# A two-layer attention trunk on one Trainium2 core: one more value product by seven half products, and its combinations of x made earlier

## Chip, core and metric

One Trainium2 chip, of which the kernel uses one core. The time is the device time of one execution in microseconds. The engines are PE (TensorE, matmuls; PEld is its weight load), DVE (VectorE), ACT (ScalarE), POOL (GpSimd) and SP (SyncE, which here only issues DMAs).

## What is computed

A trunk of two layers on 512 tokens with 1024 features, all float32. Layer 0 is a forgetting attention, layer 1 a dilated attention of three groups with eight heads each; after each layer comes an embedding step with a gate. The reference, cut to what matters:

```python
def reference(x, p, ...):
    h = x
    for i in range(2):
        if i == 0:
            h = h + fox_mixer(rms_norm(h, fox_norm[0]), fox_w_in[0], fox_b_f[0], fox_w_out[0])
        else:
            h = h + dilated_mixer(rms_norm(h, dil_norm[0]), dil_w_in[0], dil_w_out[0])
        h = h + (p[i] @ ple_w_up[i]) * jax.nn.sigmoid(h @ ple_w_gate[i])
    return rms_norm(h, final_norm)

def dilated_mixer(h, w_in, w_out):
    proj = h @ w_in                  # q, k, v of 3 groups x 8 heads x 128, then a gate z
    ...
    for g, (window, dilation) in enumerate(((128, 1), (512, 4), (2048, 16))):
        o, l = dilated_window_attention(q[:, :, g], k[:, :, g], v[:, :, g], slopes[g], window, dilation)
    ...
    return (o * jax.nn.silu(z)) @ w_out
```

## The kernel before

Every matmul of float32 operands is done as three: each operand is split into a high part (ACT rounds it to the matmul's type) and a low part (DVE subtracts), and PE adds hi x hi, hi x lo and lo x hi in PSUM.

The weights come as a stream of granules of 512 KB (class `Stream`): SP loads them into four raw buffers `wraw`, ACT and DVE split them into five slots of `whi` and `wlo`. The program is written down as a list by a Python program. A planner then sets each engine's order: of what is ready by its own estimate, it takes what was written first. So work written later can run earlier. Between the steps of a product, side work can be written: `side.push(fn, lag)` puts a function off by so many steps (`tick`), and `side.flush()` writes all that is left.

The stretch around the change, in order:

- the second matmul of layer 0's gate (16 steps, `gate_evac(1)` with `to_dil` at its end for each block b of 128 tokens). `to_dil` normalizes `h` into `xn` and pushes two `transpose_to`, which write x transposed as `xn2T` (high and low) and a plain copy `xf`. Each pushed function makes four transposes on PE, two splits and a copy.
- `up_rows(1, ...)`, the second embedding's product `p[1] @ ple_w_up[1]`: eight steps of six matmuls of 512 columns. ACT copies each step's result to a tile `upo` (three buffers) and SP stores it to `up_dram`.
- `side.flush()`; the pool `mid0` is closed (with `xn`, `upo`, `pT` and others in it), and the pool `dil` is opened on its memory.
- the dilated layer's value products for the first half of the heads, (hf, g) = (0,0), (0,1), (0,2), then the products for q and k of head after head; later (1,0), (1,1), (1,2).

A value product by `token_rows` (L302 to L304) multiplies 512 tokens with 1024 features and 512 outputs: 96 matmuls of 512 columns from four granules. By `quad_rows` (L408 to L411) it is cut into 2 x 2 blocks and made of seven half products with 24 matmuls of 256 columns each, in this order: "11", "t2", "t1", "t3", "21", "t4", "22". Each takes a block or a combination of x (`xb`) and a block or a combination of weights (`Stream.quad`: a11, s2, s1, s3, a12, a22, s4, of which the s are made on DVE in the tiles `ws` and in the raw buffer). "11" lands in a bank that ACT copies to `p1`; "21" adds to the same bank. The other results pass through DVE adds into `u2`, `u4` and `v`. The combinations of x come from `combine_x`: four subtractions in place in `xf` and four splits into `comb`. Before, (0,0) and (1,0) run by `token_rows`, the other four by `quad_rows`, and `combine_x` is pushed during (0,0).

Of the kernel before, what the change touches and what calls it, by code (L numbers as in the profile page):

```python
# [15 lines left out]
F32 = mybir.dt.float32  # L16
# [6 lines left out]
P, T, D, KT, NB = 128, 512, 1024, 8, 4  # L23
# [10 lines left out]
def trunk_kernel(ctx, tc, x, p, fox_norm, fox_w_in, fox_b_f, fox_w_out, dil_norm, dil_w_in,  # L34
# [3 lines left out]
    base = ctx.enter_context(tc.tile_pool(name="base", bufs=1))  # L38
# [4 lines left out]
    def nm(s):  # L43
        uid[0] += 1
        return f"{s}_{uid[0]}"
# [154 lines left out]
    g_fo = [tok_granules(fox_w_out[0], c * 512) for c in range(2)]  # L200
    g_g0 = [tok_granules(ple_w_gate[0], c * 512) for c in range(2)]
    g_up1 = [ws.add(ple_w_up[1], 0, 2, c * 512, 512) for c in range(2)]
    QUADS = ((0, 1), (0, 2), (1, 1), (1, 2))
    g_dv, g_dq, g_dk, g_dz = {}, {}, {}, {}
    z_after = {0: (0, 1), 2: (2, 3), 4: (4, 5), 7: (6, 7)}
    for hf in range(2):
# [38 lines left out]
    side = Side()  # L245
# [13 lines left out]
    def drive(main, steps=1, at={}):  # L259


        for i, _ in enumerate(main):
            side.tick()
            step(steps if isinstance(steps, int) else steps[i])
            if i in at:
                at[i]()
# [8 lines left out]
    def token_rows(act, granules, lhs, evac, group=1, nk=KT, halves=False):  # L275

        tiles = [None] * NB  # L280
        assert not halves or group >= len(granules)
        ng = len(granules)
        for g0 in range(0, ng, group):
            parts = {}
            for b in range(NB):
                if tiles[b] is None:
                    tiles[b] = bank(tok[b])
                end = g0 + group >= ng
                cols = ((0, 256), (256, 512)) if halves and b == NB - 1 and end else ((0, 512),)
                for c0, c1 in cols:  # L290
                    for gi in range(g0, min(g0 + group, ng)):
                        if gi not in parts:
                            parts[gi] = ws.get(granules[gi])
                        wh, wl = parts[gi]
                        if gi == 0 and c0 > 0:
                            tiles[b] = rotate(tr)
                        o = tiles[b][:, c0:c1]
                        for kk in range(2):
                            k = 2 * gi + kk
                            xh, xl = lhs(act[0], k, b), lhs(act[1], k, b)  # L300
                            first, last = k == 0, k == nk - 1
                            PE.matmul(o, xh, wh[:, kk, c0:c1], start=first, stop=False)  # L302
                            PE.matmul(o, xh, wl[:, kk, c0:c1], start=False, stop=False)  # L303
                            PE.matmul(o, xl, wh[:, kk, c0:c1], start=False, stop=last)  # L304
                        if gi == ng - 1:
                            if len(cols) > 1:
                                evac(b, o, c0, c1)
                            else:
                                evac(b, o)
                        yield  # L310
# [145 lines left out]
    def transpose_to(act, k0, b, src, copy=None):  # L456

        t = rotate(tr)
        for i in range(4):
            PE.transpose(t[:, i * P:(i + 1) * P], src[:, i * P:(i + 1) * P], ident)  # L460
        tv = t.rearrange("p (k n) -> p k n", k=4)
        split_out(act[0][:, k0:k0 + 4, b * P:(b + 1) * P],
                  act[1][:, k0:k0 + 4, b * P:(b + 1) * P], tv)
        if copy is not None:
            ACT.activation(copy[:, k0:k0 + 4, b * P:(b + 1) * P], tv, AF.Copy)
# [54 lines left out]
    def up_rows(L, pool, pT, granules):  # L520

        for c in range(2):
            def evac(b, t):
                u = pool.tile([P, 512], F32, tag="upo", bufs=(8, 3)[L], name=nm("upo"))
                ACT.activation(u, t, AF.Copy, scale=0.5)
                store = lambda c=c: SP.dma_start(up_dram[L][b][:, c * 512:(c + 1) * 512], u)
                if L == 0:
                    stores.append(store)
                else:
                    store()  # L530
            yield from token_rows(pT, [granules[c]], blk, evac, nk=2)

    stores = []
    with tc.tile_pool(name="start", bufs=1) as sp:
# [47 lines left out]
        for n, _ in enumerate(token_rows(xnT, g_v[0], blk, v_evac(0), group=4)):  # L582
# [3 lines left out]
            if n > 7:  # L586
                with tc.issue_after(last["load"].ins):
# [7 lines left out]
                       base=0, pattern=[[-1, P]], channel_multiplier=1)  # L595
    qk = base.tile([P, 8, T], F32R, tag="qkh", bufs=1, name="qk")
# [299 lines left out]
    def to_dil(b, mp, h, ss, gain, hg):  # L896
        if b == 0:
            xn2T.append(act_pair("xn2T"))
        SP.dma_start(h_dram[b], h[:, b, :])
        rstd = rstd_of(mp, ss)  # L900
        xn = mp.tile([P, D], F32, tag="xn", bufs=2, name=nm("xn"))
        DVE.scalar_tensor_tensor(xn, h[:, b, :], rstd, gain, OP.mult, OP.mult)
        for c in range(2):
            side.push(lambda c=c: transpose_to(xn2T[0], 4 * c, b, xn[:, c * 512:(c + 1) * 512], dil_in["xf"]), 10)

    mid = ExitStack()
    mp, pT1 = mid_layer(0, ozT, g_fo, g_g0, lambda b: rows(x[0])[b], fox, dil_norm, to_dil)
    drive(up_rows(1, mp, pT1, g_up1))
    side.flush()
    mid.close()  # L910


    dil = ExitStack()
    dp = dil.enter_context(tc.tile_pool(name="dil", bufs=1))
    xT = xn2T[0]

    qk = base.tile([P, 8, T], F32, tag="qkh", bufs=1, name="qk2")
    d0, d1, d2 = dil_in["dist"]
    slope = lambda g, j: 2.0 ** (-8.0 * (g * 8 + j + 1) / 24)
    scale = 128 ** -0.5  # L920

# [2 lines left out]
    comb = [a.rearrange("p k n -> p (k n)") for a in act_pair("comb")]  # L926
    for i in range(4):
        xb[f"t{i + 1}"] = [a[:, 1024 * i:1024 * (i + 1)].rearrange("p (k n) -> p k n", k=4) for a in comb]

    def by_block(d):  # L930

        return lambda h: (d.rearrange("p (b r i) -> p r b i", b=4, r=4)[:, 2 * h:2 * h + 2],
                          lambda t: t.rearrange("p (r b i) -> p r b i", r=2, b=4))

    def by_residue(d):
        return lambda h: (d[:, 256 * h:256 * h + 256], lambda t: t)

    def combine_x():

        xf = dil_in["xf"]  # L940
        b11, b12, b21, b22 = (xf[:, 4 * i:4 * i + 4, 256 * h:256 * h + 256] for i in range(2) for h in range(2))

        def less(d, a, b):
            return lambda: DVE.tensor_tensor(d, a, b, OP.subtract)

        def parts(n, d):
            return lambda: split_out(xb[n][0], xb[n][1], d)

        return [less(b11, b12, b11), less(b12, b22, b12), less(b22, b22, b11), parts("t2", b22),
                parts("t1", b11), parts("t3", b12), less(b21, b21, b22), parts("t4", b21)]  # L950

    def dil_scores(j, st):
        bias0 = dp.tile([P, 256], F32, tag="bias0", bufs=1, name=nm("bias0"))
# [144 lines left out]
    for hf in range(2):  # L1098
        v = [dp.tile([P, NB, 512], F32, tag=f"v{g}", bufs=1, name=nm("v"))
             for g in range(3)]  # L1100
        for g in range(3):
            def dv_evac(b, t, g=g, v=v):
                if b % 2 or hf == 0:
                    ACT.activation(v[g][:, b, :], t, AF.Copy)
                else:
                    DVE.tensor_copy(v[g][:, b, :], t)
            if (hf, g) in QUADS:
                drive(quad_rows(xb, g_dv[hf, g][0], dp, [ozf[:, n, :] for n in (5, 6, 7)], v[g]))
            else:
                if hf == 0:  # L1110
                    for n, piece in enumerate(combine_x()):
                        side.push(piece, 2 * n)
                drive(token_rows(xT, g_dv[hf, g], blk, dv_evac))
                if hf == 0:
                    side.flush()
                    ozf = dil_in["pool"].tile([P, 8, T], F32, tag="ozf", bufs=1, name="ozf")
            if g == 0:
                to_blocks(v[0])
        for j in range(4 * hf, 4 * hf + 4):
            st = {"q": [], "k": [], "v": v}  # L1120
            for g in range(3):
                views = []
                for n, nme in enumerate("qk"):
                    d = qk[:, 2 * g + n, :]
                    if g:
                        d = d.rearrange("p (r i) -> p r i", r=4)
                    st[nme].append(d)
                    views.append(by_residue(qk[:, 2 * g + n, :]) if g else by_block(d))
                drive(pair_rows(xb, g_dq[j, g], g_dk[j, g], dp, *views))
            if j < 7:  # L1130
                finish()
                chain.extend((dil_scores(j, st), dil_values(j, st)))
            else:
                chain.appendleft(dil_scores(j, st))
                chain.append(dil_values(j, st))
            if j in z_after:
                drive(gate_rows(*z_after[j]), (0,) + (1,) * 6)
# [59 lines left out]
```

## Time and profile before

| | |
|---|---|
| median of 3 runs | 951.77 us (951.18 to 954.47) |
| the profiled execution's own time | 950.43 us |
| its span, from the first to the last instruction | 948.7 us |
| busy: PE | 935.8 us (99%) |
| busy: PE weight loads | 843.1 us (89%) |
| busy: DVE | 698.7 us (74%) |
| busy: ACT | 500.3 us (53%) |

Times in the trace are microseconds from the start of the span. A busy time is the time in which at least one instruction of that engine is under way. Matmuls overlap, so that one of 512 columns shows 0.39 us but the next starts 0.23 us later. In the rows, "x" is a count, and the bracket at the end is the idle time before an instruction and what ended it.

### The profile page before, as it was taken

What the parts mean: (1) busy time and instruction counts of PE and PEld (TensorE: products, weight loads), DVE (VectorE), ACT (ScalarE), POOL (GpSimd) and SP (SyncE); (2) the same over time, 40 slices, a digit from 0 to 9 for tenths busy, and PEclk for the clock granted to TensorE, in tenths of its full rate; (3) what the DMA queues carried; (4) which work ended last, traced back from release to release, by engine and by line L of the source; (5) the groups of instructions that cost most, each with busy time, mean ns of one, the idle gap of its engine ahead of it and who ended that gap; (6) DMA issues with size and microseconds to landing.
All of it is one profiled execution on the core that took longest, in us unless ns stands there. A gap on an engine that the chain in (4) does not pass through costs nothing.

```text
span 948.7 us, 15802 instructions
## 1 busy us (share of the span) xinstructions
PE 935.8 (99%) x6014; PEld 843.1 (89%) x6014; DVE 698.7 (74%) x1397; ACT 500.3 (53%) x924; POOL 55.6 (6%) x119
## 2 busy tenths in 40 slices
PE   8999999999999999999999999999999999999996
PEld 7888888888888888899999999999999999998885
DVE  6856777777764478887897887758789788776456
ACT  7446776767752248533565555443356455473233
POOL 0000000000026000100000000010000000010000
PEclk9999999999999999999999999999999999999999
DMA  9352222222146227353323223335332322347102
GB/s 342 131 150 68 68 68 68 68 68 68 67 160 218 89 88 244 117 151 92 109 69 111 70 66 113 108 98 151 90 112 68 110 70 69 104 129 277 69 0 89
DMA packets 125675, 104.57 MB, mean 110 GB/s; under 512 B 14720, under 2 KB 104832, under 8 KB 125600
## 3 DMA queue, kind: packets, MB, share of 16 engines
q1 hardware_dynamic: 120096, 90.32, 31.6%
q0 software_dynamic: 4608, 12.72, 4.1%
q8 instruction: 47, 0.77, 0.3%
q10 hardware_dynamic: 896, 0.53, 0.2%
q14 instruction: 28, 0.23, 0.1%
HBM read 92.93 MB, written 10.55 MB: 109 GB/s over the span
## 4 chain that ended last, share of the span: by engine, by line
PE 93%; DVE 3%; DMA 2%; ACT 1%; issue 1%; SPq 0%; DVEq 0%; POOLq 0%; ACTq 0%
PE ps L352 9%; PE ps L351 9%; PE ps L353 9%; PE ps L302 9%; PE ps L304 9%; PE ps L303 9%; PE ps L332 5%; PE ps L334 5%; PE ps L333 5%; PE ps L408 3%; PE ps L410 3%; PE ps L411 3%; PE ps L730 2%; PE ps L460 2%; PE ps L697 2%; PE ps L1059 2%
## 5 line engine op out<-in xcount | busy, mean ns | idle before, releaser
L90 DVE TENSOR_TENSOR wlo<-wraw,whi 128x1024 fp32r<-128x1024 f32 (+1 forms) x78 | 94.3, 1211 | 99.0 <-ACT whi L88 98.7
L351 PE MATMUL ps<-comb,whi 128*128 128x256 f32 x448 | 131.2, 293 | 0.0
L88 ACT ACTIVATE whi<-wraw 128x1024 fp32r<-128x1024 f32 (+1 forms) x78 | 81.5, 1048 | 90.3 <-PE ps L304 61.9
L352 PE MATMUL ps<-comb,whi 128*128 128x256 f32 x448 | 126.9, 283 | 0.0
L353 PE MATMUL ps<-comb,wlo 128*128 128x256 f32 x448 | 126.7, 283 | 0.0
L351 PE MATMUL ps<-xn2T,whi 128*128 128x256 f32 x336 | 97.1, 289 | 0.0
L111 ACT ACTIVATE whi<-ws 128x1024 fp32r<-128x1024 f32 x56 | 59.2, 1057 | 69.4 <-PE ps L352 65.6
L353 PE MATMUL ps<-xn2T,wlo 128*128 128x256 f32 x336 | 95.1, 283 | 0.0
L352 PE MATMUL ps<-xn2T,whi 128*128 128x256 f32 x336 | 95.0, 283 | 0.0
L351 PEld LDWEIGHTS ps<-comb,whi 128*128 128x128 f32 x448 | 85.9, 192 | 0.4
L352 PEld LDWEIGHTS ps<-comb,whi 128*128 128x128 f32 x448 | 85.8, 192 | 0.4
L353 PEld LDWEIGHTS ps<-comb,wlo 128*128 128x128 f32 x448 | 85.7, 191 | 0.0
L112 DVE TENSOR_TENSOR wlo<-ws,whi 128x1024 fp32r<-128x1024 f32 x56 | 68.3, 1220 | 14.1 <-ACT whi L111 14.1
L332 PE MATMUL ps<-xnT,whi 128*128 128x512 f32 x192 | 78.5, 409 | 0.0
L334 PE MATMUL ps<-xnT,wlo 128*128 128x512 f32 x192 | 75.4, 393 | 0.0
L333 PE MATMUL ps<-xnT,whi 128*128 128x512 f32 x192 | 75.1, 391 | 0.0
L111 ACT ACTIVATE whi<-wraw 128x1024 fp32r<-128x1024 f32 (+1 forms) x56 | 46.9, 843 | 34.6 <-PE ps L352 19.3
L352 PEld LDWEIGHTS ps<-xn2T,whi 128*128 128x128 f32 x336 | 64.4, 192 | 0.0
L351 PEld LDWEIGHTS ps<-xn2T,whi 128*128 128x128 f32 x336 | 64.4, 192 | 0.0
L353 PEld LDWEIGHTS ps<-xn2T,wlo 128*128 128x128 f32 x336 | 64.3, 191 | 0.0
L112 DVE TENSOR_TENSOR wlo<-wraw,whi 128x1024 fp32r<-128x1024 f32 (+1 forms) x56 | 53.0, 951 | 2.3 <-ACT whi L111 2.0
L302 PE MATMUL ps<-whi,hT 128*128 128x512 f32 (+1 forms) x136 | 51.8, 381 | 0.0
(242 smaller groups left out, 2460.3 us busy)
## 6 DMA issues: line engine op xcount, KB each, us to landing
wraw<-in_dil_w_in_dram SPq DMA_DIRECT2D x80, 512.0 KB, 3.8
wraw<-in_fox_w_in_dram SPq DMA_DIRECT2D x32, 512.0 KB, 4.2
wraw<-in_ple_w_gate_dram SPq DMA_DIRECT2D x16, 512.0 KB, 3.8
up_dram<-upo SPq DMA_DIRECT2D x16, 256.0 KB, 5.2
wraw<-in_fox_w_out_dram SPq DMA_DIRECT2D x8, 512.0 KB, 3.4
up<-up_dram POOLq DMA_DIRECT2D x8, 512.0 KB, 6.0
wraw<-in_dil_w_out_dram SPq DMA_DIRECT2D x8, 512.0 KB, 3.5
x_in<-in_x_dram SPq DMA_DIRECT2D x4, 512.0 KB, 9.6
```

What stands on the lines that cost most here:

```text
L90: DVE.tensor_tensor(lo[:, k], t[:, k], f32(hi)[:, k], OP.subtract)
L111: ACT.activation(hi[:, :n], src, AF.Copy)
L112: DVE.tensor_tensor(lo[:, :n], src, f32(hi[:, :n]), OP.subtract)
L302: PE.matmul(o, xh, wh[:, kk, c0:c1], start=first, stop=False)
L303: PE.matmul(o, xh, wl[:, kk, c0:c1], start=False, stop=False)
L304: PE.matmul(o, xl, wh[:, kk, c0:c1], start=False, stop=last)
L332: PE.matmul(t, wh[:, k, :], xh, start=(k == 0), stop=False)
L333: PE.matmul(t, wh[:, k, :], xl, start=False, stop=False)
L334: PE.matmul(t, wl[:, k, :], xh, start=False, stop=(k == KT - 1))
L351: PE.matmul(o, ah, bh, start=(first and k == 0), stop=False, skip_group_check=not first)
L352: PE.matmul(o, ah, bl, start=False, stop=False, skip_group_check=not first)
L353: PE.matmul(o, al, bh, start=False, stop=(last and k == 3), skip_group_check=not first)
```

## The change

The value product (0,0) is made by `quad_rows`, so its weights are loaded in blocks of four by 256 columns instead of two by 512. Its three temporary tiles lie in `p0` and `p1`, which the attention of a head uses later; the other four take theirs from `ozf`, whose memory is that of `xf` and not free yet. `combine_x` is written before the second embedding's product and pushed with lags of 5 to 12, so that its pieces fall at the end of that product and the start of (0,0). The transposes of the token blocks 2 and 3 get lags of 6 and 4 instead of 10, and the flush behind the embedding's product is gone; one comes after (0,0).

```diff
-    QUADS = ((0, 1), (0, 2), (1, 1), (1, 2))
+    QUADS = ((0, 0), (0, 1), (0, 2), (1, 1), (1, 2))
...
-            side.push(lambda c=c: transpose_to(xn2T[0], 4 * c, b, xn[:, c * 512:(c + 1) * 512], dil_in["xf"]), 10)
+            side.push(lambda c=c: transpose_to(xn2T[0], 4 * c, b, xn[:, c * 512:(c + 1) * 512], dil_in["xf"]), (10, 10, 6, 4)[b])
...
-    drive(up_rows(1, mp, pT1, g_up1))
-    side.flush()
-    mid.close()
...
+    def combine_x():
+        ...
+        return [less(b11, b12, b11), less(b12, b22, b12), less(b22, b22, b11), parts("t2", b22),
+                parts("t1", b11), parts("t3", b12), less(b21, b21, b22), parts("t4", b21)]
+
+    for n, piece in enumerate(combine_x()):
+        side.push(piece, 5 + n)
+    drive(up_rows(1, mp, pT1, g_up1))
+    mid.close()
...
             if (hf, g) in QUADS:
-                drive(quad_rows(xb, g_dv[hf, g][0], dp, [ozf[:, n, :] for n in (5, 6, 7)], v[g]))
-            else:
-                if hf == 0:
-                    for n, piece in enumerate(combine_x()):
-                        side.push(piece, 2 * n)
-                drive(token_rows(xT, g_dv[hf, g], blk, dv_evac))
-                if hf == 0:
+                if hf == g == 0:
+                    temps = [t.rearrange("p b n -> p (b n)")[:, 512 * i:512 * i + 512] for t in
+                             (dp.tile([P, NB, 256], F32, tag=n, bufs=1, name=nm(n)) for n in ("p0", "p1"))
+                             for i in range(2)][:3]
+                else:
+                    temps = [ozf[:, n, :] for n in (5, 6, 7)]
+                drive(quad_rows(xb, g_dv[hf, g][0], dp, temps, v[g]))
+                if hf == g == 0:
                     side.flush()
                     ozf = dil_in["pool"].tile([P, 8, T], F32, tag="ozf", bufs=1, name="ozf")
+            else:
+                drive(token_rows(xT, g_dv[hf, g], blk, dv_evac))
```

## Rows read from the trace of the kernel before

**Rows 1.** The page, busy us, share of the span and instructions.

```profile
span 948.7 us, 15802 instructions
...
PE 935.8 (99%) x6014; PEld 843.1 (89%) x6014; DVE 698.7 (74%) x1397; ACT 500.3 (53%) x924; POOL 55.6 (6%) x119
```

**Rows 2.** Busy time of each engine in four stretches.

```profile
core 0: us, PE busy (x) PEld busy (x) DVE busy (x) ACT busy (x) POOL busy (x), PEclk, DMA share, GB/s
...
359.70:373.45 13.75, 13.75 (x74) 11.39 (x72) 12.02 (x26) 11.15 (x21) 0.00 (x0) 1.00 0.74 262
373.45:395.32 21.87, 21.87 (x100) 18.10 (x99) 19.70 (x19) 12.97 (x17) 1.38 (x3) 1.00 0.32 107
395.32:415.50 20.18, 20.11 (x167) 19.94 (x166) 15.03 (x18) 8.89 (x10) 3.27 (x6) 1.00 0.69 186
415.50:435.90 20.40, 20.40 (x172) 20.40 (x171) 16.82 (x21) 7.96 (x9) 0.00 (x0) 1.00 0.37 104
```

**Rows 3.** Timeline of PE: start, us, engine, line, operation, out<-in, shape, count.

```profile
354.72 1.04 PE L460 MATMUL ps<-ident,xn 128*128 128x128 f32 x8
...
372.66 1.03 PE L460 MATMUL ps<-ident,xn 128*128 128x128 f32 x8
373.45 0.47 PE L302 MATMUL ps<-whi,xn2T 128*128 128x512 f32 x1
...
395.32 0.28 PE L408 MATMUL ps<-whi,xn2T 128*128 128x256 f32 x1
395.43 0.28 PE L410 MATMUL ps<-wlo,xn2T 128*128 128x256 f32 x1
...
939.72 0.28 PE L304 MATMUL ps<-whi,hT 128*128 128x256 f32 x1
```

**Rows 4.** Timeline of DVE.

```profile
368.37 1.28 DVE L902 SCALAR_TENSOR_TENSOR xn<-h,rstd,gain 128x1024 f32<-128x1024 f32 x1
...
377.27 1.23 DVE L944 TENSOR_TENSOR xf<-xf 128x1024 f32<-128x1024 f32 x1
379.27 1.23 DVE L147 TENSOR_TENSOR ws<-wraw,wraw 128x1024 f32<-128x1024 f32 x1 [0.77 <-DMA up_dram<-upo]
380.41 1.22 DVE L944 TENSOR_TENSOR xf<-xf 128x1024 f32<-128x1024 f32 x1
...
401.27 0.69 DVE L419 TENSOR_TENSOR ozf<-ps,ozf 128x512 f32<-128x512 f32 x1
```

**Rows 5.** Timeline of ACT.

```profile
374.61 0.63 ACT L525 ACTIVATE upo<-ps 128x512 f32<-128x512 f32 x1
...
376.64 1.20 ACT L465 ACTIVATE xf<-ps 128x512 f32<-128x512 f32 x2 [0.42 <-DVE xn2T L441]
...
398.45 0.60 ACT L416 ACTIVATE ozf<-ps 128x512 f32<-128x512 f32 x1 [1.39 <-PE ps L411]
```

**Rows 6.** Timeline of SP's queue, the DMAs that it issues.

```profile
373.84 1.75 SPq L526 DMA_DIRECT2D up_dram<-upo  x2
390.74 10.91 SPq L73 DMA_DIRECT2D wraw<-in_dil_w_in_dram  x4
```

**Rows 7.** Groups of DVE by line: two of (0,0), then two of (0,1).

```profile
L944 DVE TENSOR_TENSOR xf<-xf 128x1024 f32<-128x1024 f32 x4 | 4.9, 1220 | 0.1
L441 DVE TENSOR_TENSOR comb<-xf,comb 128x1024 fp32r<-128x1024 f32 x4 | 4.9, 1218 | 0.0
...
L139 DVE TENSOR_TENSOR wlo<-wraw,whi 128x1024 fp32r<-128x1024 f32 x4 | 4.9, 1219 | 3.1 <-ACT whi L138 3.1
L139 DVE TENSOR_TENSOR wlo<-ws,whi 128x1024 fp32r<-128x1024 f32 x3 | 3.7, 1217 | 0.0
```

**Rows 8.** Granted clock (PEclk) in two stretches after PE's last matmul.

```profile
942.00:944.00 2.00, 0.00 (x0) 0.00 (x0) 1.72 (x11) 0.03 (x1) 0.00 (x0) 1.00 0.41 168
944.00:946.00 2.00, 0.00 (x0) 0.00 (x0) 0.72 (x2) 0.69 (x1) 0.00 (x0) 0.72 0.20 78
```

More of the change, by code (lines that the diff above doesn't have):

```diff
@@ L903, in to_dil @@
         for c in range(2):
-            side.push(lambda c=c: transpose_to(xn2T[0], 4 * c, b, xn[:, c * 512:(c + 1) * 512], dil_in["xf"]), 10)
+            side.push(lambda c=c: transpose_to(xn2T[0], 4 * c, b, xn[:, c * 512:(c + 1) * 512], dil_in["xf"]), (10, 10, 6, 4)[b])
     mid = ExitStack()
     mp, pT1 = mid_layer(0, ozT, g_fo, g_g0, lambda b: rows(x[0])[b], fox, dil_norm, to_dil)
-    drive(up_rows(1, mp, pT1, g_up1))
-    side.flush()
-    mid.close()
-    dil = ExitStack()
-    dp = dil.enter_context(tc.tile_pool(name="dil", bufs=1))
     xT = xn2T[0]
[L917 to L920, printed above, removed]
     xb = {f"{i + 1}{h + 1}": [a[:, 4 * i:4 * i + 4, 256 * h:256 * h + 256] for a in xT]
@@ L928, in trunk_kernel @@
         xb[f"t{i + 1}"] = [a[:, 1024 * i:1024 * (i + 1)].rearrange("p (k n) -> p k n", k=4) for a in comb]
[L930 to L936, printed above, removed]
     def combine_x():
@@ L950, in combine_x, with by_block, by_residue @@
                 parts("t1", b11), parts("t3", b12), less(b21, b21, b22), parts("t4", b21)]
+    for n, piece in enumerate(combine_x()):
+        side.push(piece, 5 + n)
+    drive(up_rows(1, mp, pT1, g_up1))
+    mid.close()
+    dil = ExitStack()
+    dp = dil.enter_context(tc.tile_pool(name="dil", bufs=1))
+    qk = base.tile([P, 8, T], F32, tag="qkh", bufs=1, name="qk2")
+    d0, d1, d2 = dil_in["dist"]
+    slope = lambda g, j: 2.0 ** (-8.0 * (g * 8 + j + 1) / 24)
+    scale = 128 ** -0.5
+    def by_block(d):
+        return lambda h: (d.rearrange("p (b r i) -> p r b i", b=4, r=4)[:, 2 * h:2 * h + 2],
+                          lambda t: t.rearrange("p (r b i) -> p r b i", r=2, b=4))
+    def by_residue(d):
+        return lambda h: (d[:, 256 * h:256 * h + 256], lambda t: t)
     def dil_scores(j, st):
```

## The prediction

> **What bounds the kernel now.** I read the page's busy times first. TensorE (PE) is busy for 99% of the span [rows 1], so only work taken from PE, or a pause given to it, moves the end. VectorE (DVE) with 74% is next. Then I cut the trace around the change into stretches [rows 2]: the second embedding's product (359.70 to 373.45 us), the value product (0,0) that is changed (373.45 to 395.32), and the products (0,1) and (0,2), which already run as seven half products. In each, PE is busy end to end. DVE has little room: 12.02 of 13.75, 19.70 of 21.87, 15.03 of 20.18 and 16.82 of 20.40 us. The timeline of PE shows the edges [rows 3]: four groups of eight transposes of `xn` around the embedding's product, the last at 372.66 behind its last matmul, then (0,0) at 373.45 and (0,1) at 395.32. The timelines of DVE, ACT and SP's queue show what the seven products need: combinations of x [rows 4], the last copy of x [rows 5] and the last store of the embedding's product [rows 5, 6].
>
> **Part 1, PE's own work.** (0,0) now takes 96 matmuls of 512 columns, 21.87 us of PE. Afterwards it takes 168 of 256, as (0,1) does now in 20.18 us [rows 2]. That saves **1.69 us**. It is less than the eighth that the columns shrink by (168 x 256 against 96 x 512; an eighth of 21.87 is 2.7 us), because every matmul still loads its weights: PE's weight loads are busy 19.94 of 20.18 us in (0,1), and 18.10 of 21.87 in (0,0). Two of the half matmuls start 0.11 to 0.12 us apart [rows 3]; 168 at 0.12 are 20.2. [...]
>
> **Part 2, the work for DVE and ACT.** Removed for (0,0): four splits of a raw granule into high and low part (DVE 1.22 us each, one every 1.14) and four evacuations on ACT. Added: seven splits, four sums of weights (L147, L148, L151, L159) and five evacuating adds of 0.68 [rows 4, 7]. For DVE that is 3 x 1.14 + 4 x 1.14 + 5 x 0.61 = 11.0 us more. The eight pieces of `combine_x` (four subtractions and four splits of 1.22 [rows 4, 7]) are not more, only earlier. The room in the four stretches is 1.7 + 2.2 + 5.2 + 3.6 = 12.7 us [rows 2]. So DVE can take it by 435.9 with nothing to spare, and it costs nothing if it is spread evenly. At worst it isn't: what does not fit into the first two stretches, 11.0 - 3.9 = 7.1 us, would be late at the edge of (0,0). Splits of raw weights (a11, a12, a22) can run ahead as the granules' do now, in the free slots of `whi`, so I take 0 here and leave the rest to a rival. ACT has 2.6 and 8.9 us free in the first two stretches; three splits and one copy fewer than the four of now fit: 0.
>
> **Part 3, the moved transposes.** The lags for b = 2 and 3 are shorter, so their 16 transposes stand inside the embedding's product. The number is the same, each group about 0.8 us of PE [rows 3]: 0 if `xn` is there in time. It is written for b = 3 at 368.37 to 369.65 [rows 4], before the last step of that product, so I take 0. If PE met them as early as the lag of 4 asks, after three steps of 1.4 us and two groups (359.7 + 4.2 + 1.6 = 365.5), it would stand some 4 us; the program's order is made by a planner that puts ready work first, and the four groups of now all run without idle time before them, so I give that no chance of its own.
>
> **Part 4, a wait that gets a new neighbour.** All that `quad_rows` needs beyond the split weights lies in the pool `dil`, opened after `mid0` is closed: `ws`, and for (0,0) also `p1`, `u2`, `u4` in `p0`/`p1`. In the trace the first writer of that pool is L147, the first weight sum for (0,1). It stands idle until 379.27 and is released by the DMA from `upo` to `up_dram`, the last store of the embedding's product [rows 4], although `ws` and `upo` have nothing to do with each other: I read it so that the new pool's memory is given over only when everything in the old pool is done. Now this costs PE nothing, because (0,0) uses nothing of `dil` but `v`, 18 us later. After the change (0,0) itself needs it. Of its seven products only "11" can go ahead: its weights are raw and split, its x is tokens 0 to 255. t2, t1 and t3 need sums behind L147, and "21" adds into the bank that ACT must first copy into `p1`.
>
> So PE runs "11" from 373.45 for 24 x 0.12 = 2.9 us, to 376.3, and stands. When does the store land? Now the last evacuation runs 374.61 to 375.24 [rows 5], SP's queue has passed on its store by 375.59 [rows 6], and it has landed by 379.27. Earliest afterwards: PE's last matmul of the embedding ends at about 373.4, evacuation to 374.0, the same 4.0 us to landing, 378.0. Latest: as now plus one 0.8 us delay of ACT, 380.1. I take 379.0. Then the copy into `p1` takes 0.60 (L416 now, [rows 5]) and a hop of 0.1, and "21" starts at 379.7, if the split of a12 is ready. Pause: 379.7 - 376.3 = **3.4 us** (2.4 to 4.5). Behind it: "21" to 382.6; meanwhile s1, s2 and their splits take 1.14 + 1.06 (ACT, about as long as DVE's 1.22) + 1.22 from 379.0, ready at 382.6 for t1, and t2 follows. L147 holds back, on DVE, what is queued behind it: the rest of `combine_x`, as it does now with the second subtraction (380.41, [rows 4]). If three subtractions and two splits of x come before it, as they can from the copy of x on (b = 3 now at 376.64 to 377.84 [rows 5]; four us earlier afterwards, since its transposes are), DVE goes on without another stop of PE.
>
> The raw buffers of (0,0) come free only after those sums, so the loads for (0,1) start at about 380 instead of before 374. (0,2) has its loads issued from 390.74 on [rows 6], 14 to 25 us ahead of PE, and the lead shrinks to 3 to 16 us. L147 for (0,1) would then run at about 392 to 394, with PE due at 396.9: 0 to 1.4 us of stop; I take 0.
>
> **Sum.** -1.69 + 3.4 = +1.7 us. On the profiled execution, 950.43 us (span 948.7), that is 952.1; on the median of the runs, 951.77, it is **953.4**. A measurement can tell about 0.5%, 4.8 us, from no change, so even the full gain would be too small to tell.
>
> **Rivals.**
> 1. The wait is hidden: what `dil` gives first does not wait for the store (only for tiles at the same addresses), or the store lands while "11" runs. For it: L147's idle time now is only 0.8 us [rows 4], and other waits of the same instruction are not shown. Against: it is that very store that released it. The gain of 1.69 is then kept: 950.1 to 952.
> 2. "21" is not ready (split of a12 late, or the copy queued on ACT behind other splits). PE waits for t1 until 379.0 + 3.6 = 382.6, a pause of 6.3: +4.6, 956.4.
> 3. The other side: DVE becomes the bound. L147 stands in its queue ahead of two subtractions and the splits for t1 and t2, as now ahead of the second subtraction [rows 4]. Eight pieces of 1.14 then lie between 379.0 and the second product, which starts at 388.1 instead of 382.6: 5.5 more, +7.2, 959.0. It decides against the change (over 4.8 us slower) from a total stop of 6.5 us on, that is with three such pieces late. For it: the room in rows 2 is nearly used up. Against: the planner can place L147 later.
>
> [...]
>
> **Chances.** Likeliest (one pause of 2.4 to 4.5 us, +0.7 to +2.8): 0.42. Rival 1 (-1.7 to +0.5): 0.26. Rival 2 (+2.8 to +4.7): 0.17. Rival 3 (over +4.8): 0.13. Faster by over 4.8 us, by something that I don't see: 0.02. Faster 0.02, within 0.5% 0.85, slower 0.13. The range reaches from rival 1's full gain to a little beyond rival 2: 950.0 to 957.0. It leaves out rival 3 and what lies under 950.
>
> **What would show it.** Right: PE's stretch from the first matmul of "11" to (0,1) is 23 to 24 us long, with one gap after 24 half matmuls, released by ACT (the copy into `p1`) or through L147, and L147 or that copy released by `up_dram<-upo`; the next product after the gap is "21". Part 1 is wrong if 168 half matmuls take something other than 20.2 us net of gaps; part 3, if PE waits before a transposing group for `xn`; rival 1, if there is no gap and L147 starts at once; rival 3, if there are several gaps released by DVE. A gap inside (0,1) would mean that the late loads count.

## The result and the profile after

The changed kernel takes **961.0 us** (median of 4 runs, 960.41 to 962.14) against 951.47 for the kernel before (4 runs on the same chip, 950.68 to 954.47): a ratio of 1.0106, 95% interval 1.0094 to 1.0117. It was forecast at 953.4, and the range ended at 957.0. The profiled execution took 960.44 us, its span is 9.9 us longer than that of before [rows 1].

The page of the kernel after:

```profile
span 958.6 us, 15966 instructions
...
PE 936.8 (98%) x6086; PEld 846.9 (88%) x6086; DVE 710.2 (74%) x1409; ACT 501.8 (52%) x925; POOL 55.3 (6%) x119
```

PE's busy time has not fallen but risen by 1.0 us, and its share has lost a point. Four windows of the kernel after, cut at the edges that answer to those of [rows 2] (embedding's product; (0,0); (0,1); (0,2)), and then the beginning of (0,0) in windows of 5 us:

```profile
core 0: us, PE busy (x) PEld busy (x) DVE busy (x) ACT busy (x) POOL busy (x), PEclk, DMA share, GB/s
359.70:374.20 14.50, 14.43 (x75) 11.51 (x73) 12.30 (x28) 11.67 (x24) 0.00 (x0) 1.00 0.42 162
374.20:404.75 30.55, 23.01 (x170) 22.36 (x168) 29.21 (x30) 14.77 (x17) 0.47 (x1) 0.83 0.33 104
404.75:425.25 20.50, 20.38 (x171) 20.20 (x169) 16.66 (x18) 8.39 (x9) 3.90 (x8) 1.00 0.70 206
425.25:445.41 20.16, 20.16 (x171) 20.16 (x169) 16.57 (x21) 7.96 (x9) 0.00 (x0) 1.00 0.36 105
...
373.45:380.00 6.55, 3.78 (x28) 3.39 (x27) 6.55 (x7) 5.12 (x7) 0.00 (x0) 0.98 0.31 118
380.00:385.00 5.00, 0.58 (x1) 0.29 (x1) 5.00 (x6) 1.71 (x2) 0.00 (x0) 0.50 0.00 0
385.00:390.00 5.00, 4.65 (x20) 4.50 (x21) 5.00 (x5) 3.14 (x4) 0.00 (x0) 0.50 0.49 144
```

All of the loss stands in these rows. The next products, for q and k, start at 445.41 instead of 435.90 [rows 2]: 9.5 us later, out of the 9.9 of the whole span. (0,1) and (0,2) together take 40.66 us as before (40.58). (0,0) begins 0.75 us late and takes 30.55 us instead of 21.87. 0.22 of the 0.75 stand ahead of the stage: the first group of transposes of `xn` starts at 354.94 instead of 354.72 [rows 3]. Counted from that group, the stage is 9.3 us longer. In (0,0) DVE is busy without a break up to 390, and PE does almost nothing from 380 to 385. After that it runs for 5 us at half the clock (0.50).

The timeline of PE in the kernel after shows how the 30.55 us come about:

```profile
376.95 0.28 PE L411 MATMUL ps<-whi,xn2T 128*128 128x256 f32 x1
384.40 0.58 PE L408 MATMUL ps<-whi,comb 128*128 128x256 f32 x1 [7.17 <-ACT whi L138]
385.35 0.58 PE L408 MATMUL ps<-whi,comb 128*128 128x256 f32 x1 [0.37 <-ACT whi L138]
...
386.17 0.41 PE L411 MATMUL ps<-whi,comb 128*128 128x256 f32 x1
386.38 0.41 PE L408 MATMUL ps<-whi,comb 128*128 128x256 f32 x1
...
390.00 0.28 PE L411 MATMUL ps<-whi,comb 128*128 128x256 f32 x1
390.12 0.28 PE L408 MATMUL ps<-whi,comb 128*128 128x256 f32 x1
...
445.41 0.28 PE L351 MATMUL ps<-xn2T,whi 128*128 128x256 f32 x1
```

Read the starts. The 24 half matmuls of "11" run from 374.20 at 0.12 us each; the next would be due at 377.08 and starts at 384.40: a pause of **7.32 us** (the trace's 7.17, counted from the end of the last one, and the 0.15 by which two matmuls overlap here). Then 21 half matmuls take 5.60 us, to 390.00, where 21 x 0.12 = 2.52 were due: **3.08 us** more, from a second wait of 0.37 and from starts 0.21 apart instead of 0.12. The other 123 take 14.75 us, 0.12 each. With PE's own saving of 1.7, (0,0) is longer by -1.7 + 7.3 + 3.1 = 8.7; with the 0.75 of the start that makes the 9.5.

The next product after the pause is on `comb` ("t2"), not "21", and ACT's split of a weight sum releases it. The timeline of DVE in the kernel after shows why that split was late:

```profile
371.62 2.55 DVE L924 TENSOR_TENSOR xf<-xf 128x1024 f32<-128x1024 f32 x2 [0.18 <-ACT xf L465]
...
378.64 1.22 DVE L441 TENSOR_TENSOR comb<-xf,comb 128x1024 fp32r<-128x1024 f32 x1
379.77 1.22 DVE L147 TENSOR_TENSOR ws<-wraw,wraw 128x1024 f32<-128x1024 f32 x1
380.91 1.22 DVE L441 TENSOR_TENSOR comb<-xf,comb 128x1024 fp32r<-128x1024 f32 x1
382.04 1.22 DVE L148 TENSOR_TENSOR ws<-ws,wraw 128x1024 f32<-128x1024 f32 x1
```

And ACT's, of the same kernel:

```profile
378.05 0.60 ACT L416 ACTIVATE p<-ps 128x512 f32<-128x512 f32 x1 [0.45 <-DMA up_dram<-upo]
...
383.29 2.00 ACT L138 ACTIVATE whi<-ws 128x1024 fp32r<-128x1024 f32 x2 [3.49 <-DVE ws L148]
385.20 2.93 ACT L138 ACTIVATE whi<-wraw 128x1024 fp32r<-128x1024 f32 x3
```

The last store of the embedding's product had landed by 378.05: it releases ACT's copy into `p1`. But L147 starts only at 379.77, with no idle time before it; a piece of `combine_x` stands in front of it and another between it and L148. So the pieces of x were ahead of the weight sums, and from 378.05 on the sums were not held by the store but by DVE's queue. ACT then waits 3.49 us for L148 before it can split. The split of a12, which "21" needs, is among the three at 385.20, behind those of the sums.

### The profile page after: what moved, and what is told of

Its sections match the earlier page's. It is cut to its first block, busy times and chain, and to the rows that moved or that the text cites. A ratio compares the mean times of both kernels' runs of the same rounds, so it can differ in the third digit from the quotient of the medians.

```text
span 958.6 us, 15966 instructions
## 1 busy us (share of the span) xinstructions
PE 936.8 (98%) x6086; PEld 846.9 (88%) x6086; DVE 710.2 (74%) x1409; ACT 501.8 (52%) x925; POOL 55.3 (6%) x119
## 4 chain that ended last, share of the span: by engine, by line
PE 89%; DVE 4%; DMA 2%; ACT 2%; issue 1%; SPq 0%; DVEq 0%; ACTq 0%; POOLq 0%
PE ps L351 9%; PE ps L352 9%; PE ps L353 9%; PE ps L302 8%; PE ps L304 8%; PE ps L303 8%; PE ps L332 4%; PE ps L334 4%; PE ps L333 4%; PE ps L408 4%; PE ps L410 3%; PE ps L411 3%; PE ps L730 2%; PE ps L697 2%; PE ps L1061 1%; PE ps L988 1%
## 5 line engine op out<-in xcount | busy, mean ns | idle before, releaser
L90 DVE TENSOR_TENSOR wlo<-wraw,whi 128x1024 fp32r<-128x1024 f32 (+1 forms) x74 | 89.4, 1212 | 99.9 <-ACT whi L88 99.6
L88 ACT ACTIVATE whi<-wraw 128x1024 fp32r<-128x1024 f32 (+1 forms) x74 | 77.3, 1047 | 91.6 <-PE ps L304 62.5
L111 ACT ACTIVATE whi<-wraw 128x1024 fp32r<-128x1024 f32 (+1 forms) x56 | 46.8, 843 | 34.1 <-PE ps L352 18.5
L112 DVE TENSOR_TENSOR wlo<-wraw,whi 128x1024 fp32r<-128x1024 f32 (+1 forms) x56 | 53.0, 952 | 2.2 <-ACT whi L111 2.0
L408 PE MATMUL ps<-whi,comb 128*128 128x256 f32 x160 | 46.8, 293 | 7.7 <-ACT whi L138 7.5
```

Source lines behind the costliest of these rows:

```text
L88: ACT.activation(hi[:, k], t[:, k], AF.Copy)
L90: DVE.tensor_tensor(lo[:, k], t[:, k], f32(hi)[:, k], OP.subtract)
L111: ACT.activation(hi[:, :n], src, AF.Copy)
L112: DVE.tensor_tensor(lo[:, :n], src, f32(hi[:, :n]), OP.subtract)
L408: PE.matmul(oo, xh, wh[:, k, :], start=first and r == 0 and k == 0, stop=False, skip_group_check=True)
```

## The experiments

Each kernel below is the changed kernel with the edit shown, but for what is said. The stage is read best from the time at which the first matmul for q and k starts, since by then the three value products are done in all of them: 435.92 before, 445.41 after. The first group of transposes, ahead of the stage, starts between 354.72 and 355.13 in all the kernels but e2 (355.74), so differences of a few tenths between these starts say nothing. The ratio is to the kernel before, run beside it on the same chip, with its 95% interval.

| kernel | median us (before) | ratio | q and k start at |
|---|---|---|---|
| the change | 961.0 (951.47) | 1.0106 [1.0094, 1.0117] | 445.41 |
| e1, the moves alone | 950.78 (950.92) | 0.9999 [0.9989, 1.0008] | 436.02 |
| e2, stores outside the pool | 959.91 (950.92) | 1.009 [1.0072, 1.0107] | 444.57 |
| e3, sums in the raw buffers | 954.25 (950.92) | 1.0031 [1.002, 1.0042] | 439.51 |
| e4, "21" second | 958.23 (950.92) | 1.0074 [1.0054, 1.0094] | 442.99 |
| e5, transposes in the pause | 961.34 (951.55) | 1.0104 [1.0086, 1.0122] | 443.12 |
| e6, e3 with sums on GpSimd | 960.97 (951.55) | 1.0098 [1.0085, 1.0112] | 446.00 |
| e7, no subtractions | 957.98 (951.55) | 1.0066 [1.0051, 1.0081] | 442.57 |
| e8, e6 and transposes | 962.3 (951.55) | 1.0112 [1.0097, 1.0128] | 445.46 |
| e9, e2 and e3 | 954.76 (950.6) | 1.0048 [1.0036, 1.0061] | 439.62 |
| e10, e9 without subtractions | 951.26 (950.6) | 1.0009 [1.0, 1.0018] | 435.88 |

**e1: the moves without the seven products.** (0,0) runs by `token_rows` again; the transposes and `combine_x` stay where the change put them.

```diff
-    QUADS = ((0, 0), (0, 1), (0, 2), (1, 1), (1, 2))
+    QUADS = ((0, 1), (0, 2), (1, 1), (1, 2))
...
```

> Only the moves: combine_x before the embedding's product and the shorter lags, but (0,0) by 96 matmuls of 512 columns as before. If the loss comes from the seven products at that place, this costs no more than the 0.5 to 0.75 us by which the change starts (0,0) later: 951.5 to 952.5 us. If moving the combinations of x ahead is what hurts (DVE late for the transposes, PE waiting), part of the 9.5 us stays: over 954.

Measured: no difference (0.9989 to 1.0008), and q and k start 0.1 us after those of before. So the moved transposes and combinations cost nothing by themselves; the loss comes with the seven products at this place. The moves are not quite the same here: the planner puts the transposes of b = 2 and 3 at 365.14 and 371.18, and in the kernel after at 363.61 and 368.86.

**e2: the stores taken out of the pool.** ACT writes the last halves of the embedding's product into blocks of `h` that are done with, so that the pool `dil` no longer waits for their stores.

```diff
...
-    drive(up_rows(1, mp, pT1, g_up1))
+    drive(up_rows(1, mp, pT1, g_up1, [dil_in["h"][:, i, 512 * c:512 * c + 512] for i in range(2) for c in range(2)]))
```

> The change, but the results of the embedding's product that are stored lie in finished blocks of h and not in the pool that is closed, so the new pool doesn't wait for the last store. Theory A (DVE's order: the first weight sums stand behind pieces of combine_x, because they may not start until the pool is given over): the sums still wait for the last matmul of the embedding, and the second sum comes two DVE pieces earlier, so the pause falls from 7.2 to about 4.9 us: 956 to 959. Theory B (the store itself is what PE waits for, as predicted): the pause falls to under 2 us and the clock stays: 951 to 953. Theory C (too much DVE work in that place, in any order): 960 to 961.

Measured: q and k start 0.8 us earlier, and the median is 9.0 us over that of before instead of 9.5. But this execution was late ahead of the stage already. Its timeline of PE gives the first group of transposes at 355.74, and counted from there the stage is 1.6 us shorter than in the kernel after (88.8 us against 90.5; 81.2 before):

```profile
355.74 1.04 PE L460 MATMUL ps<-ident,xn 128*128 128x128 f32 x8
```

The timeline of DVE in this kernel:

```profile
377.16 1.22 DVE L147 TENSOR_TENSOR ws<-wraw,wraw 128x1024 f32<-128x1024 f32 x1
378.30 2.35 DVE L441 TENSOR_TENSOR comb<-xf,comb 128x1024 fp32r<-128x1024 f32 x2
380.57 1.22 DVE L148 TENSOR_TENSOR ws<-ws,wraw 128x1024 f32<-128x1024 f32 x1
```

The timeline of PE in the same kernel:

```profile
382.93 0.56 PE L408 MATMUL ps<-whi,comb 128*128 128x256 f32 x1 [4.91 <-ACT whi L138]
```

L147 starts 2.6 us earlier, but two pieces of x now stand between it and L148. A pause of 4.91 stays, as theory A had it, and the granted clock is 0.62 and 0.52 in the two windows of 4 us from 382 on; the time lies above theory A's range. The wait for the store, on which the forecast had built its pause, is not what holds PE here; DVE's queue is.

**e3: the sums made where the raw weights lie.** `Stream.quad` gets an order of its own for (0,0): a22 is split right behind a11, then s1, s2 and s3 overwrite the raw buffers, so that no sum needs the new pool.

```diff
+                p22 = split(a22)
+                DVE.tensor_tensor(a22, a21, a22, OP.add)
+                DVE.tensor_tensor(a21, a11, a21, OP.subtract)
+                DVE.tensor_tensor(a11, a22, a11, OP.subtract)
+                yield split(a11)
...
```

> The change, but the weight sums of (0,0) are written into its raw buffers, so they wait for no pool and can be made during the embedding's product; p1, u2 and u4 stay in the new pool. Theory A: the sums and their splits run before the last block of x is there, the pause falls to 0 to 2 us, the clock stays up: 950 to 953. Theory B: the copy into p1 still waits for the store, but only 21 and the adds need it: a pause of up to 1.6 us, 951 to 953. Theory C: DVE's total is the same, so the pause stays near 7 us or moves ahead of (0,0): 958 to 961.

Measured: 5.9 us of the 9.5 are won at the stage; the time lies between the ranges of theories B and C. Its timeline of PE:

```profile
378.42 0.38 PE L425 MATMUL ps<-whi,xn2T 128*128 128x256 f32 x1 [1.63 <-ACT p L433]
379.52 0.39 PE L425 MATMUL ps<-whi,comb 128*128 128x256 f32 x1 [0.71 <-ACT comb L457]
...
393.34 0.38 PE L425 MATMUL ps<-whi,xn2T 128*128 128x256 f32 x1 [0.69 <-ACT v L445]
```

The three sums now run at 362.42, 366.67 and 369.32, ahead of `xn` for b = 3. Three waits of 0.7 to 1.6 us are left, and the clock is 0.74 and 0.83 between 378 and 386. The first of the waits is for ACT's copy into `p1` (L433). That copy starts at 377.79, right behind a split on ACT, without a wait for the store.

**e4: "21" second.** a12 is split right behind a11, and "21" is written behind "11".

```diff
             yield split(a11)
+            if soon:
+                yield split(a12)
...
+        if soon:
+            yield from product(b1, "21", False)
+            ACT.activation(dst(0, 0), halves(b1), AF.Copy)
...
```

> The change, but for (0,0) the split of a12 is made second and the product 21 stands second, as my prediction took it to run. It fills 2.9 us of the pause, which becomes two of some 1.6 and 2.8 us. If the clock stays up, that also gives back the 3 us at half clock: 954 to 956. If the clock falls in the second pause anyway: 957 to 959. If the split of a12 early delays the sums by as much: 960 to 961.

Measured: 2.4 us won. Its timeline of PE:

```profile
379.40 0.39 PE L411 MATMUL ps<-whi,xn2T 128*128 128x256 f32 x1 [2.09 <-ACT p L419]
385.66 0.39 PE L411 MATMUL ps<-whi,comb 128*128 128x256 f32 x1 [1.63 <-ACT whi L138]
386.60 0.39 PE L411 MATMUL ps<-whi,comb 128*128 128x256 f32 x1 [0.56 <-ACT whi L138]
```

Here is the sequence that was forecast: "21" starts at 379.40 (forecast 379.7), released by the copy into `p1`. That the time fits is in part luck: the copy does not wait for the store here, it starts right behind a split of x on ACT. 2.2 us of waits come after "21". The timeline of DVE shows that the sums are not the reason:

```profile
381.03 1.22 DVE L150 TENSOR_TENSOR ws<-ws,wraw 128x1024 f32<-128x1024 f32 x1
```

And ACT's, of the same kernel:

```profile
378.76 0.58 ACT L419 ACTIVATE p<-ps 128x512 f32<-128x512 f32 x1
384.06 0.60 ACT L423 ACTIVATE v<-ps 128x512 f32<-128x512 f32 x1 [4.72 <-PE ps L414]
384.56 1.99 ACT L138 ACTIVATE whi<-ws 128x1024 fp32r<-128x1024 f32 x2
```

The second sum is done at 382.25, but its split stands on ACT behind the copy of the result of "21", which waits 4.72 us for PE, and starts at 384.56. "21" itself takes 4.4 us instead of 2.9, because the clock falls in it (0.81 over 378 to 382, 0.76 over 382 to 386). So what is left of the loss in e4 comes from the clock and from an order on ACT that the edit made. It does not show what late sums alone would cost behind "21".

**e5: PE kept at work in the pause.** 64 transposes of `ident` into a bank that nothing reads, written behind (0,0); the planner puts 60 of them into the pause.

```diff
+                    warm = bank(7)
+                    for n in range(64):
+                        PE.transpose(warm[:, n % 4 * P:(n % 4 + 1) * P], ident, ident)
```

> The change, with 64 transposes of the identity into a free bank of PSUM, ordered into the pause behind the first half product (60 of them, some 6 us of PE). They add work that nothing needs. If the fall of the clock in that pause costs about 3 us by itself (22 half matmuls at 0.21 instead of 0.12 us and a slow start), they give it back: 957.5 to 958.5 us. If the clock costs nothing because DVE is late anyway for the next products, the time stays at 960 to 961; if they get in the way of the first product after the pause, 961 to 962.

Measured: the granted clock is 1.00 in every window from 374 to 394, as in this one:

```profile
382.00:386.00 4.00, 3.21 (x24) 2.54 (x23) 4.00 (x6) 2.83 (x3) 0.00 (x0) 1.00 0.11 21
```

The weights come as late as before (the first half matmul of "t2" at 384.28), but q and k start 2.3 us earlier. 0.1 of it this execution was ahead from the start (first group of transposes 354.82 against 354.94), so the lowered clock cost 2.2 of the 3.1 us behind the pause. The end is the same all the same. PE's list of waits (us in total, times, longest) has in this kernel, for matmuls of the heads,

```profile
PE ps L1044 <- DVE p L1025: 3.5, 3, 2.1
```

and in the kernel after, for the same line,

```profile
PE ps L1044 <- DVE p L1025: 1.2, 2, 0.9
```

2.3 us are given back there (3.5 - 1.2). What in the order of the heads makes those waits longer was not followed up.

**e6 and e8: the sums on GpSimd.** As e3, with the four sums on the engine that is nearly idle (6% on the page). e8 has 24 transposes in the pause besides.

```diff
-                DVE.tensor_tensor(a22, a21, a22, OP.add)
+                POOL.tensor_tensor(a22, a21, a22, OP.add)
...
```

> The kernel with the weight sums of (0,0) in the raw buffers, but made by GpSimd, so DVE has four instructions of 1.14 us less. If DVE's amount of work is the bound in that place, the pauses of that kernel (1.6, 0.7 and 0.7 us, and the clock that fell in them) shrink to under 1.5 us together: 950 to 951.5 us, about 3 us less than with DVE. [...]

> The kernel with the sums on GpSimd and 24 transposes of the identity that fill what pauses PE still has there. If the clock still falls in its pauses, this gives back 0.5 to 1.5 us against the kernel without them; if the clock stays up there, it is the same or up to 1 us slower.

Measured: all of e3's gain is lost; 960.97 lies 9.5 us above the end of the range expected of e6 for the case that DVE's amount of work is the bound. In e8 the transposes keep the clock at 1.00 from 374 to 406 (in e6 it is 0.50 over 386 to 390), but q and k start only 0.5 us earlier, and the median is 1.3 us higher than e6's, outside both ranges expected. The timeline of GpSimd in e6:

```profile
365.17 2.35 POOL L149 TENSOR_TENSOR wraw<-wraw,wraw 128x1024 f32<-128x1024 f32 x1
367.60 3.22 POOL L150 TENSOR_TENSOR wraw<-wraw,wraw 128x1024 f32<-128x1024 f32 x1
```

The timeline of DVE in e6:

```profile
362.76 2.35 DVE L502 SCALAR_TENSOR_TENSOR rstd<-rstd 128x1 f32<-128x1 f32 x1
365.03 0.68 DVE L458 TENSOR_TENSOR xn2T<-ps,xn2T 128x512 fp32r<-128x512 f32 x1
365.63 2.97 DVE L919 SCALAR_TENSOR_TENSOR xn<-h,rstd,gain 128x1024 f32<-128x1024 f32 x1
368.52 2.84 DVE L857 TENSOR_TENSOR h<-h,th 128x512 f32<-128x512 f32 x1
```

The timeline of PE in e6:

```profile
368.75 1.94 PE L477 MATMUL ps<-ident,xn 128*128 128x128 f32 x8 [3.85 <-DVE xn L919]
```

While GpSimd adds (one of its sums of 128x1024 takes 3.22 us), DVE's L919 takes 2.97 us instead of 1.28 (at 375.94, without an add beside it); L857, 0.69 us in e3, takes 2.84; and L502, on a single column, takes 2.35 instead of 0.16 (at 360.71 in e6). That is 6.0 us more on these three, against 4 x 1.14 = 4.6 us for the sums that DVE was spared, and `xn` comes 3.85 us late for PE.

**e7: the four subtractions of `combine_x` left out.** This part of the computation is missing here: the combinations are uncombined blocks of x. DVE has 4 x 1.14 us less to do.

```diff
-            return lambda: DVE.tensor_tensor(d, a, b, OP.subtract)
+            return lambda: None
```

> The change without the four subtractions of combine_x (t1 to t4 are then splits of plain blocks of x, which leaves that part of the computation out). DVE has four instructions of 1.14 us less in the stretch, nothing else changes. If DVE's amount of work sets the pause (7.2 us), it shrinks by 3.4 to 4.5 us, too short for the clock to fall: 952 to 954. If the pause is the wait for the pool (store landed at 378, then two sums and a split), it shrinks by 2 to 2.5 us and the clock may still fall: 955 to 959. If neither, 960 to 961.

Measured: 2.8 us won, with the granted clock at 0.73 and 0.50 in the two windows of 4 us from 378 on. The timeline of ACT in this kernel:

```profile
377.64 0.60 ACT L416 ACTIVATE p<-ps 128x512 f32<-128x512 f32 x1 [1.26 <-DMA up_dram<-upo]
```

The timeline of DVE in this kernel:

```profile
377.68 1.23 DVE L147 TENSOR_TENSOR ws<-wraw,wraw 128x1024 f32<-128x1024 f32 x1
...
379.02 1.22 DVE L148 TENSOR_TENSOR ws<-ws,wraw 128x1024 f32<-128x1024 f32 x1
```

The timeline of PE in this kernel:

```profile
381.38 0.58 PE L408 MATMUL ps<-whi,comb 128*128 128x256 f32 x1 [4.25 <-ACT whi L138]
```

With the subtractions out of the way, L147 starts as soon as the store has landed (by 377.64), and the pause is 4.25: the pool until 377.7, two sums and a split. DVE is done with the piece ahead of L147 at the same moment (377.64), so 4.25 is what the store alone costs, and what DVE's shorter queue alone would cost as well. In the kernel after the other 2.9 of the 7.17 are the pieces of x in front of L147 (1.7 from the store's landing at 378.05 to 379.77) and between it and L148 (1.1). The two causes lie one behind the other, and e2 shows that to take the first away alone only makes more room for the second.

**e9 and e10: both mended, then less work for DVE.** e9 joins the edits of e2 and e3; e10 leaves out the subtractions besides, with e7's edit.

> The stored halves of (0,0) taken from finished blocks outside the dilated layer's buffers, and the weight sums formed in the buffers of the raw weights, so that the split of a22 can run ahead. Theory A (the pause has two causes in a row, the buffers given over late and the sums behind VectorE's pieces of x): with both gone no wait of TensorE at the start of product (0,0) is over 1.5 us, the granted clock there stays at 0.9 or more, and the time is 951 to 953.5 us against some 951.2 before. Rival B (VectorE's amount of work alone binds: sums, splits and combinations keep it full from 365 to 390 us): waits of 0.5 to 2 us move to the normalised block b = 3 and to the combined pieces, and the time stays at 953.5 to 955 us, as with the sums in the raw buffers alone.

> The run with both mendings, and the four subtractions of combine_x left out as well (this part of the computation is left out: the combined operands are the uncombined ones), so that VectorE has some 4.6 us less to do. Theory A with VectorE's amount as the remainder: no pause is left, the 1.7 us of TensorE's work show, 949 to 950.8 us against some 951.2 before. Rival C (the seven products don't save TensorE time at this place even when fed, because of the moved transposes or the order of the planner): 951.5 to 953.5 us.

Measured: e9 is no better than e3, so theory A falls, and the time is that of rival B. The timeline of DVE in e9:

```profile
371.47 1.29 DVE L921 SCALAR_TENSOR_TENSOR xn<-h,rstd,gain 128x1024 f32<-128x1024 f32 x1
```

The timeline of ACT in e9:

```profile
376.94 1.06 ACT L138 ACTIVATE whi<-wraw 128x1024 fp32r<-128x1024 f32 x1
377.91 0.58 ACT L433 ACTIVATE p<-ps 128x512 f32<-128x512 f32 x1
```

The timeline of PE in e9:

```profile
378.54 0.38 PE L425 MATMUL ps<-whi,xn2T 128*128 128x256 f32 x1 [1.63 <-ACT p L433]
```

`xn` for b = 3 is written at 371.47 instead of 368.37 [rows 4], with the three sums ahead of it on DVE (the last at 369.44). ACT's copy into `p1` starts right behind a split, with no wait for the store, and PE waits 1.63 us for it. It was so in e3 already (377.79), and so to take the store away as well changes nothing. Of the waits that rival B named, only the one for a combined piece of x is there (0.71 us at 379.63); the longest is that for ACT's copy. The timeline of PE in e10:

```profile
378.18 0.39 PE L425 MATMUL ps<-whi,comb 128*128 128x256 f32 x1 [1.31 <-ACT xf L482]
```

In e10, with 4.6 us less on DVE, this one wait of 1.31 us is left, the clock is 1.00 in all windows from 360 to 430, and q and k start at 435.88, where they start before. From the first group of transposes (354.83) the stage takes 81.05 us, and 81.20 before; net of the wait it is 1.5 us shorter, near the 1.69 of part 1. So the seven products do save PE time here; even when DVE is given 4.6 us that it can't have, a wait of 1.3 us eats it. e10's median, 951.26, lies between the two ranges expected, and its 0.7 us over that of before arise behind the stage: in the profiled executions PE waits 2.1 us in the heads for DVE, and 0.8 before.

## Why the prediction was wrong

- **The step that failed** is in part 4: "21" would fill the wait, "if the split of a12 is ready", and "DVE goes on without another stop of PE". The first rests on part 2's sentence that the splits of raw weights can run ahead. Only a11's did (357.68). In the code a12's split stands behind those of s2, s1 and s3, and "21" behind t2, t1 and t3; that the place decides, e4 shows, which moves both: "21" starts at 379.40. Which of the two places counts, and why the planner left them as written, no run shows. The second failed with the pieces of x on DVE, 1.7 us ahead of L147 and 1.1 between it and L148. The pause was 7.3 us instead of 3.4, and the lowered clock and a second wait added 3.1.
- **What came is nearest to rival 2**: "21" not ready, and PE waits for the next product. Its pause of 6.3 became 7.3, and it had no price for the clock. It also named t1 as that product; by the program's order it is t2, which takes s2 and so both sums. The price from L147 to that product, 3.6, was about right all the same (e7: 377.68 to 381.38).
- **The store** landed by 378.05 (forecast 378.0 to 380.1), and the copy into `p1` waited for it as forecast. That number is right by luck: the last evacuation ended at 375.86 (375.28 + 0.58) instead of 374.0, and the landing took at most 2.2 us behind it instead of 4.0. As the only price of the pause the store was wrong: e2 takes it away and the stage wins 1.6 us.
- **DVE's work** was counted right (11.0 us more; the page shows 11.5) and then valued at nothing. The 7.1 us that did not fit into the first two stretches were named as the worst case; DVE ran full from 371.62 to 390. The mechanism of rival 3 was the right engine with the queue the other way round: it had L147 stand ahead of the pieces of x, and in fact they stood ahead of L147 and L148. That its price, +7.2, lies nearest to the 9.5 measured is chance, since the 9.5 hold 3.1 us behind the pause that no rival had priced. e3 (5.9 us won by earlier sums) shows that DVE's order decides, and e10 that in the end its room does.
- **The clock** has no term in the sum, and no rival has a price for it. In the kernel after it is 0.98 over 373.45 to 380, and 0.50 over 380 to 385. An estimate from these two rows: 0.02 x 6.55 / 0.5 = 0.26 us at 0.50, so that it fell at about 379.7, 2.5 us after the end of the last matmul (376.95 + 0.28). By that the pause of 3.4 us that was forecast would have lasted longer than the clock did here. Of the 3.1 us behind the pause, 2.2 are the clock's (e5).
- **Part 1** was right: without waits, a half matmul every 0.12 us, 20.2 us for 168, 1.7 less than before. **Part 3** was right to some tenths: with the moves alone (e1) q and k start 0.1 us late. In the kernel after, PE does wait for `xn`, which part 3 gave as its sign of being wrong: the transposes of b = 2 and 3 start at 363.61 and 368.86, 0.14 and 0.15 us after `xn` is written, and hold PE up by some 0.4 us together. The late loads for (0,1) cost nothing: (0,1) and (0,2) run as before.

## What to carry to other kernels

Before PE's work is exchanged for vector work, lay out the vector engine's queue over the stretch in which the first results are due, not over the whole: here 12.7 us of room in four stretches hid a lack of 7 us in the first two. A wait that a planner fills with ready work is not free: what is waited for then stands behind the filling, so of two causes in a row the removal of one can win little (e2: 1.6 of the 9.3 us at the stage). The same holds for an engine's queue: in e4 a copy that waits for PE keeps a ready split behind it for 2.3 us. And the pause of PE had a second price here, the matmuls behind it at the lower clock: 2.2 us (e5).

## What the runs showed of the hardware

- **The clock fell some time after PE's last matmul, and came back some time after PE's return.** In the kernel after it fell about 2.5 us after the last matmul (the estimate above). In the tail of the kernel before it is 0.72 in a stretch of 2 us [rows 8] and 0.50 from there to the end of the span (946.00 to 948.70); by these two it was 1.1 us at 0.50 in the first, so it fell some 4.9 us after the last matmul's end (an estimate). In the kernel after it was back at 390.00, 5.6 us after matmuls had begun again: 0.50 over 385 to 390, and from 390.00 on half matmuls start 0.12 us apart. In e3 it fell (0.74 between 378 and 382) though no rest was longer than 1.63 us. In e4 (0.81 between 378 and 382, by the same estimate 1.5 us at 0.50) it fell at about 380.5, when PE had been at work again since 379.40. In e10 a rest of 1.31 us left it at 1.00. So in e4 the end of the rest did not keep the clock up; how long a rest may be without a fall, these runs do not settle.
- **GpSimd's adds held VectorE up in e6.** The three instructions of DVE that began while one of the adds of this stretch ran and took longer are L919 (2.97 us instead of 1.28), L857 (2.84 instead of 0.69) and L502, on a single column (2.35 instead of 0.16). The one that reads PSUM took its usual 0.68 beside them (365.03), and L856, begun 0.04 us ahead of the first add, its usual 0.69 (362.15). The three seem to wait for the add to end: L502 ends 0.02 us after the add beside it (362.19 + 2.90), L919 1.08 and L857 0.54 after theirs, each within its own usual time. GpSimd's three adds of this stretch took 2.35 to 3.22 us; no run has one with DVE idle, so what DVE costs them is not shown, and neither is the cause of the waits.
